# Moving a whole filter network, four d-tiles' transposes and two weight loads ahead of the first modulation

## The chip, the core and the metric

The kernel runs on one core of one Trainium2 chip. The metric is device microseconds of that core. PE is TensorE (PEld its weight loads), DVE is VectorE, ACT is ScalarE, POOL is GpSimd, SP is SyncE, which here only issues DMAs. All times below are in microseconds (us) unless ns is written.

## What is computed

Two layers over 512 latent tokens and 256 context tokens of width 1024. The first is a Hyena layer: a modulated norm, an input projection to four streams of 2048 channels, a short convolution, a long convolution by FFT with an implicit filter that a small network makes, a gate, and an output projection. The second is grouped-query attention. Cut to what this change touches:

```
sh, sc, gt = split(silu(c) @ ada_w[i] + ada_b[i], 3)
h_lat = rms_norm(x_lat, norm_g[i]) * (1 + sc) + sh          # the same for the context with c_ctx
proj  = h @ w_in                                            # (L, 1024) @ (1024, 8192)
h = sin(freq * (z @ w1 + b1)); h = sin(freq * (h @ w2 + b2)); h = sin(freq * (h @ w3 + b3))
k = (h @ w4) * decay                                        # 768 rows of z: the lags of both sequences
y = irfft(rfft(x1 * v) * rfft(k / sum|k|)); y = (y + u * d) * x0 * silu(z)
```

## The kernel before

Channels lie on partitions, tokens on the free axis: d-tile k holds 128 of the 1024 model channels for 512 + 256 tokens. Every product of two full-precision operands is split into a rounded high part and a remainder, and made of three matmuls (high by high, high by low, low by high). So `in_step` takes one d-tile of the projection with six matmuls: three of 512 latent columns (`pl`) and three of 256 context columns (`pc`).

The order of work is the order in which the code is written, sorted by a scheduler that gives each engine one fixed list; no engine passes an instruction that waits. `issue_after` (in `after`) only orders two instructions.

The start of the program does this. Small inputs come as rows (4 loads on SP, 15 on POOL's queue, `zt` among them) and are turned on PE (`ptr`). SP then loads two pieces of the modulation's weights, the 12 half tiles of x and ctx, and the other pieces. `load_x` also squares a half tile on ACT for the norm. `mlp_layer(li)` is one layer of the filter's network: a matmul, seven DVE operations over 768 columns of 64 partitions in two pieces (`ma`, `mn`), and a sine on ACT. Layer 0 runs at the start; layers 1 and 2 run inside `begin`. `ada0(dh, k)` are the matmuls of half dh of the modulation's columns (`prow`); `ada0_cols` copies them (`srow`), turns them (`padc`) and adds the bias (`ada`, `gsc`).

`begin` then writes the modulated d-tiles: for each k it turns x on PE (`xT`), applies scale and shift on ACT (`hf`), casts the latent high part on DVE and the context's on ACT, and subtracts for the low parts (`h_lo` on DVE, `hc_lo` on POOL). Two d-tiles behind, it runs `in_step` for two channel tiles, 16 (weights `whi`, `wlo`) and 32 (`fw`), with the second half of the modulation between. The low parts of weights are 1024 wide subtractions on POOL (`load_w`). The six `lags` of a group of 256 channels are the matmuls `pk` of the network's output by w4, multiplied by the decay on DVE into `kfl` and `kfc`.

After `begin`, eight groups g run: two `u_stage`, a `z_stage`, an `x0_stage` with the spectra's products (`ab..`, `Y..` on DVE, from PE's `pu`), a `z_stage`, and a last `x0_stage`, into whose eight steps the lags of group g + 1 are written:

```
x0_stage(g, 1, [none, fi[0], none, none, fi[1], fi[2], lambda: run(fi[3:5]), lambda: run(fi[5:7])])
```

`fi[1]` to `fi[6]` are the six lags. Tiles from `axt` (`xT`, `pk`, `pu`, `ks`, `pq`) share four PSUM banks in turn, so the fourth lag writes the bank of the last `pu`, which `ab..c` on DVE must have read. `ks` are the filter's DFTs (first `ks0m`); their operands F, Fh and Fl are made on POOL and ACT.

Of the kernel before, what the change touches and what calls it, by code (L numbers as in the profile page):

```python
# [19 lines left out]
P = 128  # L20
# [32 lines left out]
def hybrid_kernel(ctx: ExitStack, tc: tile.TileContext, x, c, ctxt, c_ctx, norm_g, ada_w, ada_b,  # L53
                  hy_w_in, hy_conv_w, hy_conv_b, fw1, fb1, fw2, fb2, fw3, fb3, fw4, freq, hy_d,
                  hy_w_out, at_w_in, at_q_g, at_k_g, at_w_out,
# [42 lines left out]
    lo_default, w_last = [G], [None]  # L98
# [8 lines left out]
    def load_w(src, shape, scale_row=None, lo_eng=None, st=None, more=None, behind=None):  # L107
# [14 lines left out]
        with after(behind) if behind else ExitStack():  # L122
            S.copy(hi, st)  # L123
# [6 lines left out]
    vb = gp.tile([P, NA + NB + NC_], F32, tag="vb", name="vb")  # L130
    conv_w_rows = hy_conv_w.rearrange("a k (t p) -> (a k t) p", p=P)
    conv_b_rows = hy_conv_b.rearrange("a (t p) -> (a t) p", p=P)
    d_rows = hy_d.rearrange("a (t p) -> (a t) p", p=P)
# [76 lines left out]
    hc_done = []  # L210

    def h_write(pt, s, k):

        hi, lo, w, en = (h_hi, h_lo, LL, V) if s == 0 else (hc_hi, hc_lo, LC, G)
        t = cvtile(f"hf_{s}_{k}")
        sa = S.activation(t[:, :w], pt[:, :w], AF.Identity, bias=col_sh(0, s, k), scale=col_gsc(0, s, k))
        if s:
            sa = S.copy(hi[:, k, :], t[:, :w])
        else:
            V.tensor_copy(hi[:, k, :], t[:, :w])  # L220
        r = en.tensor_tensor(lo[:, k, :], t[:, :w], f(hi[:, k, :]), ALU.subtract)
        if s:
            hc_done.append(r)
        return sa

# [15 lines left out]

    rows = hp.tile([P, T], F32, tag="y", name="rows")
    rowsA, rowsB, rowsC = rows[:, 0:P], rows[:, P:2 * P], rows[:, 2 * P:3 * P]
    nc.sync.dma_start(rowsA[16:24], c.rearrange("a (t p) -> (a t) p", p=P))
    nc.sync.dma_start(rowsA[24:32], c_ctx.rearrange("(t p) -> t p", p=P))
    nc.sync.dma_start(rowsA[0:16], norm_g.rearrange("l (t p) -> (l t) p", p=P))
    nc.sync.dma_start(rowsA[32:80], ada_b.rearrange("l (t p) -> (l t) p", p=P))
    zt = f(wp.tile([P, 1024], F32R, tag="wlo", name="zt", bufs=NWB))[0:33, 0:T]
    G.dma_start(zt, k_z)
    w1, w2, w3, bc = rows[0:33, 384:448], rows[0:64, 448:512], rows[0:64, 512:640], rows[:, 640:644]  # L250
    G.dma_start(w1, fw1[0])
    for i, b in ((0, fb1), (3, freq), (1, fb2), (2, fb3)):
# [12 lines left out]
    V.tensor_copy(vb[:, 0:NA], ptr[:, 0:NA])
# [17 lines left out]
    def mlp_layer(li, behind=None, pe_behind=None):  # L283

        w, cur, kdim, m = (w1, w2, w3)[li], feat[0], 64 if li else 33, P if li == 2 else 64
# [69 lines left out]
    def ada0(dh, k, behind=None):  # L355
# [3 lines left out]
        for x_, t in enumerate(ad_st.pop((dh, k))):  # L359
            q = (k % 2 * 2 + x_) * 32  # L360
            with after(behind) if behind else ExitStack():
                TE.matmul(prow[dh][q:q + 32, :], silp[:, 2 * k:2 * k + 32], t, start=k < 2, stop=k >= KD - 2)

    def ada0_cols(dh, behind=None):
        srow = cvtile(f"srow{dh}")
        sr = S.copy(srow[:, 0:512], prow[dh])
# [1047 lines left out]
```

## Time and profile before

| | |
|---|---|
| three timed runs | 1491.02 median, 1490.41 to 1492.36 |
| the profiled execution, timed | 1493.28 |
| its span in the profile | 1491.5 |
| PE busy | 1443.6 (97%) |
| DVE, ACT, POOL busy | 1086.2, 560.4, 500.1 |

The span is the time from the first to the last instruction of the profiled execution; its timed value has 1.8 around that. PE's busy time holds some waiting of pipelined matmuls. PEclk is the clock that TensorE was granted, as a share of its full speed. Rows below give the start, then the length, both in us, then engine, line, operation, what is written and what is read; in brackets stands the idle time of that engine just before, and what ended it.

### The profile page before, as it was taken

The numbers are of one execution on the slowest core, as the hardware profiler recorded it, in microseconds if no ns is written. First come the engines' busy times: TensorE is split into PE (matmuls) and PEld (weight loads), VectorE is DVE, ScalarE is ACT, GpSimd is POOL, SyncE is SP. The second block draws the span as 40 slices with busy tenths as digits, with TensorE's granted clock in tenths as the row PEclk, the third lists the DMA queues.
The fourth block names the chain that finished last, engine by engine and source line by source line (L and its number), as shares of the span: only waits on it lengthen the run. The fifth ranks groups of instructions, "written<-read, shape, count | busy, mean of one in ns | idle before, by whom it ended". The sixth has DMA issues, their size and how long they took to land.

```text
span 1491.5 us, 23805 instructions
## 1 busy us (share of the span) xinstructions
PE 1443.6 (97%) x9274; PEld 1260.5 (85%) x9274; DVE 1086.2 (73%) x1907; ACT 560.4 (38%) x1096; POOL 500.1 (34%) x452
## 2 busy tenths in 40 slices
PE   5799999999999999999999999999999999999998
PEld 2588888888888888888897878799998998998987
DVE  4668959678596785977858454656787878878886
ACT  5232332423323233232233343534445444445442
POOL 4363543635436255372554351211110000000005
PEclk9799999999999999999999999999999999999999
DMA  9511332323323233232222775255222312312111
GB/s 327 157 47 54 113 104 67 117 64 114 107 64 110 75 113 102 64 112 79 82 73 71 287 259 192 73 155 174 93 93 72 99 43 71 99 44 71 57 56 72
DMA packets 177601, 157.51 MB, mean 106 GB/s; under 512 B 7128, under 2 KB 155179, under 8 KB 176977
## 3 DMA queue, kind: packets, MB, share of 16 engines
q1 hardware_dynamic: 173136, 134.75, 29.4%
q0 software_dynamic: 4208, 20.72, 4.0%
q8 instruction: 73, 1.20, 0.3%
q10 hardware_dynamic: 144, 0.52, 0.1%
q14 instruction: 40, 0.32, 0.1%
HBM read 138.13 MB, written 17.84 MB: 105 GB/s over the span
## 4 chain that ended last, share of the span: by engine, by line
PE 72%; DVE 14%; DMA 2%; POOL 1%; issue 1%; ACT 1%; SPq 0%; ACTq 0%; POOLq 0%; DVEq 0%
PE po L71 3%; PE po L72 3%; PE po L70 3%; DVE Y L644 3%; PE et L1210 3%; PE pq L691 3%; PE plx L518 3%; PE plx L522 2%; PE plx L519 2%; PE px L70 2%; PE px L71 2%; PE px L72 2%; PE pq L70 2%; PE pq L72 2%; PE pq L71 2%; PE pz L71 2%
## 5 line engine op out<-in xcount | busy, mean ns | idle before, releaser
L124 POOL TENSOR_TENSOR wlo<-stg,whi 128x1024 fp32r<-128x1024 f32 x65 | 159.3, 2451 | 214.8 <-ACT whi L123 214.2
L123 ACT CAST whi<-stg 128x1024 fp32r<-128x1024 f32 x99 | 104.0, 1051 | 256.4 <-issue 180.5
L969 POOL TENSOR_TENSOR r2q<-s2q,mhalf 128x2 f32<-128x2 f32 x32 | 23.1, 722 | 343.8 <-DVE s2q L967 343.8
L1198 ACT ACTIVATE E<-sc,st 128x768 f32<-128x768 f32 x64 | 57.7, 902 | 127.0 <-DVE st L1196 126.9
L518 PE MATMUL plx<-h_hi,whi 128*128 128x512 f32 x248 | 101.2, 408 | 0.0
L522 PE MATMUL plx<-h_hi,wlo 128*128 128x512 f32 x248 | 98.3, 397 | 0.0
L519 PE MATMUL plx<-h_lo,whi 128*128 128x512 f32 x248 | 98.0, 395 | 0.0
L1195 DVE TENSOR_REDUCE st<-sc 128x1 f32<-128x768 f32 x64 | 61.0, 953 | 17.3 <-PE sc L72 17.0
L520 PE MATMUL pcx<-hc_hi,whi 128*128 128x256 f32 x248 | 69.8, 282 | 0.0
L521 PE MATMUL pcx<-hc_lo,whi 128*128 128x256 f32 x248 | 69.8, 281 | 0.0
L523 PE MATMUL pcx<-hc_hi,wlo 128*128 128x256 f32 x248 | 69.7, 281 | 0.0
L1215 DVE TENSOR_TENSOR ptl<-et,pth 128x768 fp32r<-128x768 f32 x64 | 61.0, 954 | 5.2 <-ACT pth L1214 3.2
L848 DVE TENSOR_TENSOR yl<-yf,yh 128x768 fp32r<-128x768 f32 x26 | 26.0, 1002 | 52.2 <-ACT yh L847 51.8
L1214 ACT CAST pth<-et 128x768 fp32r<-128x768 f32 x64 | 51.1, 799 | 31.1 <-PE et L1210 31.0
L520 PEld LDWEIGHTS pcx<-hc_hi,whi 128*128 128x128 f32 x248 | 46.8, 189 | 11.4
L521 PEld LDWEIGHTS pcx<-hc_lo,whi 128*128 128x128 f32 x248 | 46.8, 189 | 11.0
L72 PE MATMUL po<-pth,kvt 128*128 128x256 f32 x192 | 54.1, 282 | 0.0
L70 PE MATMUL po<-pth,kvt 128*128 128x256 f32 x192 | 54.1, 282 | 0.0
L71 PE MATMUL po<-ptl,kvt 128*128 128x256 f32 x192 | 53.9, 281 | 0.0
L518 PEld LDWEIGHTS plx<-h_hi,whi 128*128 128x128 f32 x248 | 46.9, 189 | 8.2 <-issue 0.2
L1210 PE MATMUL et<-ident,E 128*128 128x128 f32 x384 | 52.3, 272 | 0.0
L518 PE MATMUL plz<-h_hi,whi 128*128 128x512 f32 x128 | 52.0, 406 | 0.0
(917 smaller groups left out, 5124.1 us busy)
## 6 DMA issues: line engine op xcount, KB each, us to landing
stg<-in_hy_w_in_dram SPq DMA_DIRECT2D x64, 512.0 KB, 4.2
stg<-in_at_w_in_dram SPq DMA_DIRECT2D x40, 512.0 KB, 4.3
adw<-in_ada_w_dram SPq DMA_DIRECT2D x32, 512.0 KB, 3.9
yf<-y_scr POOLq DMA_DIRECT2D x32, 384.0 KB, 5.3
stg<-in_hy_w_out_dram SPq DMA_DIRECT2D x16, 512.0 KB, 6.7
stg<-in_at_w_out_dram SPq DMA_DIRECT2D x16, 512.0 KB, 3.5
dec<-in_k_dec_dram SPq DMA_DIRECT2D x48, 128.0 KB, 2.5
y_scr<-y SPq DMA_DIRECT2D x16, 384.0 KB, 3.2
```

What stands on the lines that cost most here:

```text
L70: TE.matmul(ps, lh, rh, start=first, stop=False)
L71: TE.matmul(ps, lh, rl, start=False, stop=False)
L72: TE.matmul(ps, ll, rh, start=False, stop=last)
L123: S.copy(hi, st)
L124: (lo_eng or lo_default[0]).tensor_tensor(lo, st, f(hi), ALU.subtract)
L518: TE.matmul(pl, hi[:, k, :], h_hi[:, k, :], start=fi, stop=False)
L519: TE.matmul(pl, hi[:, k, :], h_lo[:, k, :], start=False, stop=False)
L520: TE.matmul(pc[:, 0:LC], hi[:, k, :], hc_hi[:, k, :], start=fi, stop=False)
L521: TE.matmul(pc[:, 0:LC], hi[:, k, :], hc_lo[:, k, :], start=False, stop=False)
L522: TE.matmul(pl, lo[:, k, :], h_hi[:, k, :], start=False, stop=la)
L523: return TE.matmul(pc[:, 0:LC], lo[:, k, :], hc_hi[:, k, :], start=False, stop=la)
L1210: TE.transpose(tp_[:, b * P:(b + 1) * P], E[:, b * P:(b + 1) * P], ident)
```

## The change

- Small inputs: the host hands in `cols` (all vectors as columns, 128x292) and `fws` (the network's three weights), and with the positions `zt` three loads on SP take the place of the 19; the turning on PE goes.
- Loads on SP: all of x and ctx first, then the first half of the modulation's weights with the weights of channel tile 16 inside, then those of tile 32, w4 of group 0, and the second half.
- The network: layers 0 and 1 put their 768 columns as 384 columns on 128 partitions (two matmuls side by side on PE, one DVE operation where there were two). All three layers run before the modulation's columns are made.
- `keep_x` turns d-tiles 0 to 3 before the modulation is known and keeps them raw in SBUF; scale and shift are then applied in place. The first weights are cast to their high part before the columns, too.
- The context's high part is cast on DVE, not on ACT.
- `begin` runs the second tile one d-tile behind the first, with the rest of the modulation between.
- For group 0, the filter's DFTs and sums are ordered behind other work (by `after`).
- Of the six lags of each later group, the last two move into the next group's first stage (words 4 and 5 of `steps`), and the four others come one in each step.

```diff
-    hc_done = []
-    def h_write(pt, s, k):
-        hi, lo, w, en = (h_hi, h_lo, LL, V) if s == 0 else (hc_hi, hc_lo, LC, G)
-        t = cvtile(f"hf_{s}_{k}")
-        sa = S.activation(t[:, :w], pt[:, :w], AF.Identity, bias=col_sh(0, s, k), scale=col_gsc(0, s, k))
-        if s:
-            sa = S.copy(hi[:, k, :], t[:, :w])
-        else:
-            V.tensor_copy(hi[:, k, :], t[:, :w])
-        r = en.tensor_tensor(lo[:, k, :], t[:, :w], f(hi[:, k, :]), ALU.subtract)
-        if s:
-            hc_done.append(r)
+    hc_done, u_done = [], []
+    def h_write(k, src, behind=None):
+        t = raw.get(k)
+        if t is None:
+            t = cvtile(f"hf{k}")
+        for s, hi, lo, c_, en in ((0, h_hi, h_lo, slice(0, LL), V), (1, hc_hi, hc_lo, slice(LL, T), G)):
+            with after(behind) if behind else ExitStack():
+                sa = S.activation(t[:, c_], src(s), AF.Identity, bias=col_sh(0, s, k), scale=col_gsc(0, s, k))
+            V.tensor_copy(hi[:, k, :], t[:, c_])
+            r = en.tensor_tensor(lo[:, k, :], t[:, c_], f(hi[:, k, :]), ALU.subtract)
+        hc_done.append(r)
         return sa
+    raw = {}
...
-    nc.sync.dma_start(rowsA[16:24], c.rearrange("a (t p) -> (a t) p", p=P))
...
+    nc.sync.dma_start(vb, cols)
...
+    fw = hp.tile([P, T], F32, tag="y", name="fw")[:, 0:256]
+    nc.sync.dma_start(fw, fws)
+    nc.sync.dma_start(zt, k_z)
+    sil_done = S.activation(sil, vb[:, 16:32], AF.Silu)
...
-    def mlp_layer(li, behind=None, pe_behind=None):
...
+    def mlp_layer(li, behind=None, v_behind=None):
+        cur, m = feat[0], P if li == 2 else 64
...
-        for lo_, hi_ in ((0, 512), (512, 768)):
-            pp = axt(f"mlp{li}_{lo_}")
-            with after(pe_behind) if pe_behind else ExitStack():
-                mm = TE.matmul(pp[:m, 0:hi_ - lo_], w[:kdim, :m], cur[:kdim, lo_:hi_], start=True, stop=True)
-            aa, nn = a[:m, lo_:hi_], n[:m, lo_:hi_]
-            V.tensor_scalar(aa, pp[:m, 0:hi_ - lo_], bc[:m, li:li + 1], bc[:m, 3:4], ALU.add, ALU.mult)
+        for hh in range(2):
+            if li == 2 or not hh:
+                pp = axt(f"mlp{li}_{hh}")
+            r_ = slice(hh * 64, hh * 64 + 64)
+            lh, rh = ((fw[0:33, 0:64], cur[:, hh * 384:hh * 384 + 384]) if li == 0 else
+                      (fw[r_, 64 * li:64 * li + m], cur[r_, 0:384]))
+            mm = TE.matmul(pp[0:m, 0:384] if li == 2 else pp[r_, 0:384], lh, rh, start=True, stop=True)
+            if li < 2 and not hh:
+                continue
+            o_ = slice(hh * 384, hh * 384 + 384) if li == 2 else slice(0, 384)
+            aa, nn = a[:, o_], n[:, o_]
+            with after(v_behind) if v_behind else ExitStack():
+                V.tensor_scalar(aa, pp[:, 0:384], bc[:, li:li + 1], bc[:, 3:4], ALU.add, ALU.mult)
...
+    def turn_x(k):
+        pts = [axt(f"xT{k}_{s}") for s in range(2)]
+        for s, pt in enumerate(pts):
+            for t in range(4 if s == 0 else 2):
+                src = halves[(t + 4 * s) * 2 + k // 4][:, (k % 4) * P:(k % 4 + 1) * P]
+                TE.transpose(pt[:, t * P:(t + 1) * P], src, ident)
+        return pts
+    def keep_x(k):
+        t = raw[k] = cvtile(f"raw{k}")
+        pts = turn_x(k)
+        V.tensor_copy(t[:, LL:T], pts[1][:, 0:LC])
+        return S.copy(t[:, 0:LL], pts[0])
...
+    for i in range(12):
+        load_x(i)
+    for k in range(6):
         ada0_load(0, k)
-    sqs = [load_x(i, None if i else sil_done) for i in range(8)]
+    st16 = wp.tile([P, 1024], F32, tag="stg", name="stg16", bufs=NST)
+    nc.sync.dma_start(st16.rearrange("p (k e) -> p k e", k=KD), load_first(16))
+    for k in range(6, KD):
+        ada0_load(0, k)
+    st32 = wp.tile([P, 1024], F32, tag="stg", name="stg32", bufs=NST)
+    nc.sync.dma_start(st32.rearrange("p (k e) -> p k e", k=KD), load_first(32))
+    w4s0 = load_w4(0)
+    for k in range(KD):
+        ada0_load(1, k)
+    sqs = [square_x(i, None if i else sil_done) for i in range(6)]
     _, l0, s0 = mlp_layer(0, sqs[-1])
-    sqs += [load_x(i, None if i > 8 else s0) for i in range(8, 12)]
-    for k in range(2, KD):
-        ada0_load(0, k)
-    for k in range(2):
-        ada0(0, k)
+    sqs += [square_x(i, s0) for i in range(6, 10)]
+    m1, l1, s1 = mlp_layer(1, sqs[-1], l0)
+    sqs += [square_x(i, s1) for i in range(10, 12)]
     sv = ss.rearrange("p (t i) -> p t i", i=2)
-    with after(l0):
+    with after(l1):
         V.tensor_tensor(sv[:, :, 0], sv[:, :, 0], sv[:, :, 1], ALU.add)
     r0 = rms_rstd(sv[:, :, 0], 6, "r0", kg)
+    for k in range(2):
+        ada0(0, k, m1)
     for i in range(12):
         if i % 2:
             xs = S.activation(halves[i], halves[i], AF.Copy, scale=r0[:, i // 2:i // 2 + 1])
         else:
-            V.tensor_scalar(halves[i], halves[i], r0[:, i // 2:i // 2 + 1], None, ALU.mult)
+            xv = V.tensor_scalar(halves[i], halves[i], r0[:, i // 2:i // 2 + 1], None, ALU.mult)
+    m2, l2, s2 = mlp_layer(2)
     for k in range(2, KD):
+        if k < 6:
+            kx = keep_x(k - 2)
         ada0(0, k)
...
+    first_w = {16: load_w(None, (KD, P), st=st16, behind=kx)}
+    sr = ada0_cols(0, s2=s2)
...
-        AHEAD, sa, lags = 2, None, []
-        for k0_ in (0, 4):
-            for i in range(4 + AHEAD):
-                k = k0_ + i
-                if k == 1:
-                    ws.append(load_w(None, (KD, P), st=st32, behind=sa,
-                                     more=lambda i: [hp.tile([P, 1024], F32R, tag="AB", name=f"fw{x}", bufs=NAB)
-                                                     for x in range(2)]))
...
-                if i >= AHEAD:
-                    for e, w in zip(es, ws):
-                        last = in_step(w, *begun[e], k - AHEAD)
-                    if k0_ == 0:
-                        for k1 in (2 * (i - AHEAD), 2 * (i - AHEAD) + 1):
-                            ada0(1, k1, last)
-                if k0_ == 0 and i > 3:
-                    mlp_layer(i - 3, sa, last)
-                if k0_ and i:
-                    for _ in range(1 if i < 5 else 2):
-                        lags.pop(0)()
-            if k0_ == 0:
-                ada0_cols(1)
...
-                first_w[17] = load_w(hy_w[:, 17 * P:18 * P].rearrange("(k p) e -> p k e", p=P), (KD, P), behind=sa)
-                lags += kfilter(0, sa)
+        ws.append(load_w(None, (KD, P), st=st32, behind=sr,
+                         more=lambda i: [hp.tile([P, 1024], F32R, tag="AB", name=f"fw{x}", bufs=NAB) for x in range(2)]))
+        fw_cast, lags, pts = w_cast[0], [], {}
+        def write(k):
+            if k in raw:
+                return h_write(k, lambda s: raw[k][:, 0:LL] if s == 0 else raw[k][:, LL:T], None if k else fw_cast)
+            if k not in pts:
+                pts[k] = turn_x(k)
+            return h_write(k, lambda s: pts[k][s][:, 0:LL if s == 0 else LC])
+        for i in range(5):
+            if i < 4:
+                sa = write(i)
+            for e, w, k in zip(es, ws, (i, i - 1)):
+                if 0 <= k < 4:
+                    cur[0] = in_step(w, *begun[e], k, cur[0])
+            for k1 in ((0, 1), (2, 3), (4, 5), (6,), (7,))[i]:
+                cur[0] = ada0(1, k1, cur[0])
+            if i == 1:
+                lags += kfilter(0, sa, w4s0)
+        for _ in range(2):
+            lags.pop(0)(cur[0])
+        ada0_cols(1)
+        pts[4] = turn_x(4)
+        for i in range(6):
+            if i < 4:
+                sa = write(4 + i)
+            if i == 1:
+                first_w[17] = load_w(load_first(17), (KD, P), behind=sa)
+            for e, w, k in zip(es, ws, (i - 1, i - 2)):
+                if 0 <= k < 4:
+                    cur[0] = in_step(w, *begun[e], 4 + k)
+            if i and lags:
+                lags.pop(0)()
...
-    steps = (("m - y - - a - -", "- - Mp - Y - a -", "- - Po - - a - -", "- n Oc - N - a -", "- - C - a - - -"),
+    steps = (("m 4 y 5 - a - -", "- - Mp - Y - a -", "- - Po - - a - -", "- n Oc - N - a -", "- - C - a - - -"),
...
-        x0_stage(g, 1, [none, fi[0], none, none, fi[1], fi[2], lambda: run(fi[3:5]), lambda: run(fi[5:7])])
+        x0_stage(g, 1, [none, fi[0], none, none] + fi[1:5])
+        late += fi[5:]
```

On PE, this is before: layer 2 of the network (`mlp`) stands behind the second half of the modulation (`prow`), inside `begin`, and the columns (`padc`) behind it.

```order
L362 MATMUL prow_363<-ad_7_0_291,silp 32x512
L362 MATMUL prow_363<-ad_7_1_292,silp 32x512
L291 MATMUL mlp_0_456<-ma_416,rows 128x512
L291 MATMUL mlp_512_466<-ma_416,rows 128x256
L369 MATMUL padc_482<-sel_131,srow_480 128x4 x4
L565 MATMUL ptr_491<-ident,rows 128x128
```

And this is the start of PE's list now; `prow_239` is the first half of the modulation, `xT_0_283` the first kept d-tile.

```order
L275 MATMUL mlp_0_205<-zt,fw 64x384 x2
L275 MATMUL mlp_0_222<-ma_203,fw 64x384 x2
L352 MATMUL prow_239<-ad_0_139,silp 32x512 x2
L275 MATMUL mlp_0_258<-ma_220,fw 128x384
L275 MATMUL mlp_1_268<-ma_220,fw 128x384
L352 MATMUL prow_239<-ad_1_141,silp 32x512 x2
L352 MATMUL prow_239<-ad_2_0_143,silp 32x512
L352 MATMUL prow_239<-ad_2_1_144,silp 32x512
L378 MATMUL xT_0_283<-ident,x_117 128x128
```

All three layers have moved ahead of nearly the whole first half, and the transposes stand between its pieces.

On ACT, the rows around the first modulated d-tiles before (`srow_253` is the copy of the first half's columns):

```order
L366 COPY srow_253<-prow_220 128x512
L216 ACTIVATE hf_0_304<-xT_0_299,ada_83,gsc_85 128x512
L123 CAST whi_265<-stg_264 128x1024
L216 ACTIVATE hf_0_311<-xT_1_308,ada_83,gsc_85 128x256
L216 ACTIVATE hf_1_324<-xT_0_319,ada_83,gsc_85 128x512
```

and now (`ma_256` are the two sines of layer 2):

```order
L386 COPY raw_282<-xT_0_283 128x512
L288 ACTIVATE ma_256<-ma_256 128x384
L386 COPY raw_295<-xT_0_296 128x512
L386 COPY raw_308<-xT_0_309 128x512
L288 ACTIVATE ma_256<-ma_256 128x384
L386 COPY raw_321<-xT_0_322 128x512
L121 CAST whi_338<-stg_159 128x1024
L358 COPY srow_342<-prow_239 128x512
L217 ACTIVATE raw_295<-raw_295,ada_83,gsc_85 128x512
L121 CAST fw_357<-stg_169 128x1024
L217 ACTIVATE raw_282<-raw_282,ada_83,gsc_85 128x512
```

The copy of the columns now stands behind layer 2's sines, the four raw copies and the first weight cast; d-tile 0 (`raw_282`) is modulated behind the cast of the second weights.

At the end of a group, PE's list had the third and the fourth lag together ahead of the last d-tile of the projection:

```order
L432 MATMUL pk_2_1329<-w4h_1279,h_135 128x512
L433 MATMUL pk_2_1329<-w4l_1280,h_135 128x512
L432 MATMUL pk_3_1336<-w4h_1279,h_135 128x512
L433 MATMUL pk_3_1336<-w4l_1280,h_135 128x512
L518 MATMUL plx_1_1262<-h_hi,whi_1257 128x512
L519 MATMUL plx_1_1262<-h_lo,whi_1257 128x512
```

and has the fourth behind it now:

```order
L461 MATMUL pk_2_1288<-w4h_1238,h_116 128x512
L462 MATMUL pk_2_1288<-w4l_1239,h_116 128x512
L551 MATMUL plx_1_1221<-h_hi,whi_1216 128x512
L552 MATMUL plx_1_1221<-h_lo,whi_1216 128x512
L553 MATMUL pcx_1_1222<-hc_hi,whi_1216 128x256
L554 MATMUL pcx_1_1222<-hc_lo,whi_1216 128x256
L555 MATMUL plx_1_1221<-h_hi,wlo_1217 128x512
L556 MATMUL pcx_1_1222<-hc_hi,wlo_1217 128x256
L461 MATMUL pk_3_1301<-w4h_1238,h_116 128x512
```

So six matmuls of the projection now lie between the two lags.

## Rows read from the trace of the kernel before

**Rows 1.** The page: busy us of each engine, share of the span, instructions.

```profile
PE 1443.6 (97%) x9274; PEld 1260.5 (85%) x9274; DVE 1086.2 (73%) x1907; ACT 560.4 (38%) x1096; POOL 500.1 (34%) x452
```

**Rows 2.** Busy us by stretch: PE, PEld, DVE, ACT, POOL; granted clock, DMA, GB/s.

```profile
50.70:53.70 3.00, 0.05 (x5) 0.01 (x1) 2.47 (x7) 1.80 (x4) 1.58 (x1) 1.00 0.28 75
53.70:74.10 20.40, 15.46 (x49) 11.44 (x50) 15.23 (x29) 6.71 (x13) 6.03 (x5) 0.50 0.20 59
74.10:82.90 8.80, 8.80 (x51) 7.68 (x51) 5.62 (x7) 4.45 (x8) 4.28 (x6) 0.99 0.16 46
82.90:122.10 39.20, 35.29 (x213) 31.24 (x212) 26.57 (x42) 14.06 (x23) 27.88 (x25) 0.96 0.19 55
153.30:1491.50 1338.20, 1321.02 (x8631) 1168.69 (x8631) 986.08 (x1747) 504.26 (x991) 431.23 (x380) 1.00 0.33 101
```

**Rows 3.** PE's waits over the span: us in total, times, longest.

```profile
PE ptr L263 <- DMA rows<-in_ada_b_dram: 4.5, 1, 4.5
PE mlp L291 <- ACT ma L300: 3.0, 1, 3.0
PE pk L432 <- DVE ab21c L635: 1.1, 1, 1.1
```

**Rows 4.** Timeline, the start of the program.

```profile
7.40 2.79 PE L291 MATMUL mlp<-zt,rows 33*64 33x512 f32 x4 [2.55 <-DMA rows<-in_hy_fw_dram]
10.03 1.25 DVE L293 TENSOR_SCALAR ma<-mlp,rows 64x512 f32<-64x512 f32 x2 [4.69 <-DMA rows<-in_hy_freq_dram]
...
15.61 0.61 DVE L298 TENSOR_SCALAR ma<-ma 64x512 f32<-64x512 f32 x2
...
16.95 0.92 ACT L300 ACTIVATE ma<-ma 64x512 f32<-64x512 f32 x2
...
19.26 0.63 ACT L322 ACTIVATE sq<-xutl 128x512 f32<-128x512 f32 x1
...
20.77 0.17 DVE L392 TENSOR_TENSOR ss<-ss 128x6 f32<-128x6 f32 x1 [4.54 <-ACT sq L322]
...
22.71 1.28 DVE L398 TENSOR_SCALAR x<-x,r 128x512 f32<-128x512 f32 x3 [1.57 <-POOL r L207]
...
25.18 1.32 ACT L396 ACTIVATE xutl<-xutl,r 128x512 f32<-128x512 f32 x2
...
27.79 0.58 ACT L366 COPY srow<-prow 128x512 f32<-128x512 f32 x1 [1.29 <-PE prow L362]
...
30.01 0.78 ACT L216 ACTIVATE hf<-xT,ada,gsc 128x512 f32<-128x512 f32 x1 [1.64 <-PE xT L548]
...
30.69 1.04 ACT L123 CAST whi<-stg 128x1024 fp32r<-128x1024 f32 x1
...
31.29 0.69 DVE L221 TENSOR_TENSOR h_lo<-hf,h_hi 128x512 fp32r<-128x512 f32 x1
...
31.78 0.50 PE L518 MATMUL pl<-h_hi,whi 128*128 128x512 f32 x1 [0.28 <-ACT whi L123]
```

**Rows 5.** Timeline, POOL and DVE at the split of the second weights.

```profile
34.17 0.93 POOL L221 TENSOR_TENSOR hc_lo<-hf,hc_hi 128x256 fp32r<-128x256 f32 x1
...
35.05 2.82 POOL L124 TENSOR_TENSOR fw<-stg,fw 128x1024 fp32r<-128x1024 f32 x1
...
35.56 2.59 DVE L220 CAST h_hi<-hf 128x512 fp32r<-128x512 f32 x1
```

**Rows 6.** Timeline of PE in begin.

```profile
47.38 0.50 PE L518 MATMUL pl<-h_hi,whi 128*128 128x512 f32 x1
...
49.67 1.07 PE L362 MATMUL prow<-ad,silp 128*32 128x512 f32 x8
...
69.47 0.79 PE L519 MATMUL pl<-h_lo,whi 128*128 128x512 f32 x1 [1.13 <-DVE h_lo L221]
```

**Rows 7.** Timeline at the end of group 0: PE, then DVE.

```profile
153.26 0.50 PE L432 MATMUL pk<-w4h,h 128*128 128x512 f32 x1 [1.04 <-DVE ab01c L635]
...
151.99 1.22 DVE L635 TENSOR_TENSOR ab01c<-pu,kt0c 128x1024 f32<-128x1024 f32 x1
```

More of the change, by code (lines that the diff above doesn't have):

```diff
@@ L361, in ada0, with ada0_cols @@
             with after(behind) if behind else ExitStack():
-                TE.matmul(prow[dh][q:q + 32, :], silp[:, 2 * k:2 * k + 32], t, start=k < 2, stop=k >= KD - 2)
-    def ada0_cols(dh, behind=None):
+                mm = TE.matmul(prow[dh][q:q + 32, :], silp[:, 2 * k:2 * k + 32], t, start=k < 2, stop=k >= KD - 2)
+        return mm
+    def ada0_cols(dh, behind=None, s2=None):
         srow = cvtile(f"srow{dh}")
-        sr = S.copy(srow[:, 0:512], prow[dh])
+        with after(s2) if s2 else ExitStack():
+            sr = S.copy(srow[:, 0:512], prow[dh])
         padc = axt(f"padc{dh}")
@@ L425, in kfilter, with lags @@
         kfs[g] = (kl, kc)
-        def lags(tl):
+        def lags(tl, behind=None):
             dc = k0.tile([P, 256], F32, tag="dec", name=f"dec{g}_{tl}", bufs=2)
@@ L431, in lags @@
             hs = h3[:, tl * P:(tl + 1) * P]
-            TE.matmul(pk, hs, wh, start=True, stop=False)
+            with after(behind) if behind else ExitStack():
+                TE.matmul(pk, hs, wh, start=True, stop=False)
             TE.matmul(pk, hs, wl, start=False, stop=True)
@@ L439, in lags @@
                 V.memset(dst[0:1, 256:512], 0.0)
-        return [lambda tl=tl: lags(tl) for tl in range(6)]
+        return [lambda behind=None, tl=tl: lags(tl, behind) for tl in range(6)]
     def knorm(g):
@@ L447, in knorm @@
             mx = kg.tile([P, 256], F32, tag="mx", name=f"mx{g}_{si}", bufs=2)
-            V.tensor_reduce(mx, src.rearrange("p a (s c) -> p c (a s)", s=2), AX.X, ALU.add,
-                            apply_absolute_value=True)
+            with after(u_done[0]) if not g else ExitStack():
+                V.tensor_reduce(mx, src.rearrange("p a (s c) -> p c (a s)", s=2), AX.X, ALU.add,
+                                apply_absolute_value=True)
             mxs.append(mx)
@@ L480, in kdft @@
                 c0, c1, d0, d1 = src[:, hf], src[:, hb], src[:, hf], src[:, hb]
-            G.tensor_tensor(F[:, 0:256], c0, c1, ALU.add)
-            G.tensor_tensor(F[:, 256:512], d0, d1, ALU.subtract)
+            with after(hc_done[-1]) if not g else ExitStack():
+                G.tensor_tensor(F[:, 0:256], c0, c1, ALU.add)
+                G.tensor_tensor(F[:, 256:512], d0, d1, ALU.subtract)
             if nm == "p" and par == 0:
@@ L497, in finish @@
                     Fh, Fl = banks[par]
-                    mm3(pt[:, r_], kmat[0][:, mset, par, cs, :], kmat[1][:, mset, par, cs, :],
-                        Fh[:, r_], Fl[:, r_], True, True)
+                    with after(cur[0]) if not g else ExitStack():
+                        mm3(pt[:, r_], kmat[0][:, mset, par, cs, :], kmat[1][:, mset, par, cs, :],
+                            Fh[:, r_], Fl[:, r_], True, True)
                 pts.append(pt)
@@ L514, in hybrid_kernel, with in_step @@
     hy_w = hy_w_in[0]
-    def in_step(w, pl, pc, k):
+    def in_step(w, pl, pc, k, behind=None):
         (hi, lo), fi, la = w, k == 0, k == KD - 1
-        TE.matmul(pl, hi[:, k, :], h_hi[:, k, :], start=fi, stop=False)
+        with after(behind) if behind else ExitStack():
+            TE.matmul(pl, hi[:, k, :], h_hi[:, k, :], start=fi, stop=False)
         TE.matmul(pl, hi[:, k, :], h_lo[:, k, :], start=False, stop=False)
@@ L527, in spread @@
             it()
-    begun = {}
+    begun, cur = {}, [None]
     def begin(es):
@@ L577, in in_proj @@
         for k in range(KD):
[L578 removed]
+            cur[0] = in_step(w, pl, pc, k)
             spread(items, k)
@@ L776, in slots @@
             table = {"n": kn[0], "N": kn[1], "a": ada_next, "-": none, "y": lambda: [y() for y in ya],
-                     "Y": lambda: [y() for y in yb]}
+                     "Y": lambda: [y() for y in yb], "4": lambda: late.pop(0)(), "5": lambda: late.pop(0)()}
             for i in range(4):
```

95 lines of the change are left out of this document (34 added, 61 removed).

## Prediction

> **What bounds the kernel now.** Read the page first: PE is busy 1443.6 of 1491.5 us [rows 1], so it bounds the kernel, and only its 47.9 idle and its time at a low clock can be won; no edit here takes much work from it. Then the table of stretches [rows 2]: behind 153.3 PE idles 17.2 of 1338.2 us, so the rest, about 30.7, lies in the start. There the reader sees three holes. PE stands still from 50.7 to 53.7, its clock falls to 0.50 and stays there to 74.1, and inside that it idles another 4.9; from 82.9 to 122.1 it idles 3.9. Then the waits [rows 3]: the hole at 50.7 is layer 2 of the network, waiting for layer 1's sine, and behind the start the one wait that repeats is that of the fourth lag for `ab..c`, about 1.1 us, one for each of the seven groups that prepare a next one. So two questions decide: when does PE reach a common point (I take the first matmul of group 0's x0 stage, where the stretch of [rows 2] ends at 122.1; behind it both kernels have the same work), and what becomes of the seven waits.
>
> **1. Layers 0 and 1.** The network can start when the third load on SP has landed. Before, PE's first wait ended at 4.5 with the fourth small load on that queue [rows 3]; I take 4.5. A layer's matmuls took 2.8 for 768 columns [rows 4]. Now two pieces of 384 columns write different halves of PSUM's partitions. If they run together, they take 1.4, if in turn 2.8. The nearest row is the modulation's, where four full-precision matmuls (two records each) of 512 columns that write four strips take 1.07 together [rows 6], so I take 1.4. DVE's seven steps over 768 columns ran from 10.0 to 16.2 [rows 4], half as many columns 3.1; a sine takes 0.46, hand-overs 0.3. Layer 0 ends at 4.5 + 5.3 = 9.8, layer 1 at 15.0 or so.
> The Trainium skill (TensorEngine Tiling (Array Packing), Key Properties) says that different tiles of the array execute in parallel, but also that changing the tiling mode drains the engine. With the first alone the layers take 1.4 each, in turn 2.8 each and the sum below would be 2.8 worse; no row of before shows two half arrays.
>
> **2. The norm.** The last two squares now wait for layer 1's sine on ACT. Two took 1.5 (19.26 to 20.77 [rows 4]): 16.5. But DVE's list has both first steps of layer 2 (0.63 each) around the sum of squares, and the second needs the second matmul, at 15.0 + 2.8 = 17.8. So the norm's factor starts at 18.5, and from the sum to the first scaling were 1.94 (20.77 to 22.71), so 1.75 more: scaling starts at 20.2, against 22.71. DVE scales six half tiles at 0.43, to 22.8; ACT six, which took 3.8 (22.71 to 26.50), to 24.0.
>
> **3. ACT becomes the path.** Layer 2's first sine waits for 3.5 of DVE work behind the scalings: 26.3. Behind it in ACT's list stand another sine, three raw copies (0.58, as `srow`), and the first weight cast (1.04): the columns' copy starts at 30.0, not at 27.79. The modulation's matmuls, which the loads held up before, are done by then. From that copy to the first modulated tile took 2.2 (27.79 to 30.01), so 32.2.
>
> **4. The first matmul.** ACT now modulates d-tile 1 (0.78), casts the second weights (1.04), then modulates d-tile 0 (0.78): 34.8. DVE's cast of it then meets POOL's split of those weights, begun at 34.1. In the row of before such a cast took 2.59 and ended with POOL's 2.82 [rows 5]; a pass of that width not held takes 0.43 (the scalings [rows 4]). I take the held one: `in_step` starts at 36.9 (35.2 if not held), 5.1 later than before (31.78).
> The Trainium skill (SBUF — State Buffer, on the shared port pair) says the pair is an exclusive lock for a whole instruction. It speaks against the change, which also gives DVE the context's casts; by it the eight new casts may each wait for a POOL split, which my sum takes once, and once in step 6.
>
> **5. First half of begin.** d-tile 0 also needs DVE's subtraction (0.69 [rows 4]), the context's cast (0.3, an estimate from 0.43 for twice its columns) and POOL's subtraction (0.93 [rows 5]): its six matmuls end at 39.1. Then seven `in_step` at 1.15 (two between 47.38 and 49.67 [rows 6]) and four groups of `prow` at 1.0: 51.1. PE has idled from about 31 to 36.9, and before, 3.0 of idling were followed by the clock of 0.50, which came back at 74.1, after 4.6 us of dense work from 69.47 [rows 2, 6]. So 4.6 us at half rate cost 2.3: 53.4. Before, this point was 50.7; the change is 2.7 behind here.
>
> **6. Second half of begin.** From 50.7 to 82.9 PE did 0.05 + 15.46 / 2 + 8.80 = 16.6 us of work at full clock [rows 2], of which 1.4 was layer 2 (half of layer 0's 2.8, an estimate), now done. 15.2 remain, and 1.5 for POOL's split of tile 17's weights, which stands ahead of d-tile 5's `hc_lo` in POOL's list: 70.1, against 82.9. Between the halves the columns' copy, `padc`, a modulated tile and its cast follow on each other, 2.2 + 0.78 + 0.43 = 3.4; PE has two lags, `padc` and two d-tiles' transposes meanwhile, so I count no hole; without that cover it is 3.4.
>
> **7. To the x0 stage.** From 82.9 to 122.1 PE was busy 35.3; the DFTs now come seven d-tiles later, which gives POOL and ACT the time to make their operands. I leave 0.8 for one wait of the old kind: 106.2 against 122.1. The start gives **15.9**.
>
> **8. The lags.** PE was free at 152.2, `ab01c` ended at 153.2, and the fourth lag began at 153.26 [rows 7]. With one `in_step` (1.05 to 1.15) ahead of it the wait is 0.1 at most. The last two lags come among the next stage's matmuls, in banks that DVE left long before; each of the six later groups gains alike: **7.0**. The loads of decay for them are issued when DVE leaves their buffers, as before.
>
> The sum is 22.9 from the profiled execution's 1493.3, which gives 1470.4. The median lies 2.3 below that execution, so I predict **1468**. The other edits cost or give nothing that I can see: 16 loads fewer, since SP's stream of large loads ends ahead of steps 3 to 5; w4's earlier load; the order among group 0's DFTs, for which PE has work of the projection.
>
> **Bounds.** Up: no fall of the clock 2.3, no held cast 1.8, no wait at tile 17 1.5 and none in step 7 0.8, the lags whole 0.6, so 7.0 better: 1461. Down: the layers' matmuls in turn 2.8, two more casts held 4.8, half of the lags' gain lost 3.5, so 11.1 worse: 1479.
>
> **Rivals.**
> - *DVE and POOL bind begin.* POOL's splits and `w4l` stand among the `hc_lo`, and DVE has more casts. For it: 4.9 idle in the old second half, waiting for such tiles. Against it: DVE needs 0.43 + 0.69 + 0.3 for a d-tile, PE 2.3. One more hold of 2.4 for each of three splits gives 1475, with the other low bounds up to 1480.
> - *The lags only move their wait.* DVE's products end just when the wait ends [rows 7], so they are as late for whatever needs them next. Then only the start is won: 1475. Against it: the banks behind the fourth lag's go to `pq` and the moved lags, the first of them two `in_step` later.
> - *The start is better still,* if neither clock nor cast holds it: 1461 by the bounds, and down to 1455 where begin packs closer than its old rows.
> - *Slower: the clock stays low.* From 36.9 to 70.1 PE has 27 us of work at full rate, with small pieces between. At half rate through all of it the start costs 25 more than I count, which cancels the gain; beyond that point, into the 35 us of step 7, the kernel is slower, 1503 if ten more go so. For it: the row of 53.7 to 74.1, where 15.46 of 20.4 were busy and the clock stayed down. Against it: what ran there was little but layer 2, columns, transposes and waits, and 4.6 us of `in_step` brought it back. The Trainium skill (TensorE: Matmul & The Clock Gate, Part 1) says the same of idling and of sustained work.
>
> **How the numbers follow.** My forecast, 1463 to 1474, has 0.55. Bound begin or a moved wait (1474 to 1482) has 0.27, the better start 0.13, a low clock through begin and on 0.03, no effect 0.02. From 1460 to 1480 leaves out some 0.06 below and 0.09 above. A measurement of this kernel tells 0.2%, 3 us, from no change: faster 0.95, same 0.02, slower 0.03.
>
> **What would show it.** In the new profile: layer 1's sine ends near 15; scaling starts near 20; the first `in_step` near 37, behind a DVE cast that ends with POOL's split; clock 0.50 from the thirties to the early forties; the first DFT `ks0m` near 78 without a long wait; the x0 stage's first matmul near 106; no wait of `pk` for `ab..c` over 0.2. I am wrong if PE waits for `hc_lo` or `h_lo` through begin, if the clock stays down beyond 45, or if another wait of about 1 us stands once in each group.

## The result: 13.6 us slower

The changed kernel took 1504.31 us (median of four runs, 1502.51 to 1507.34) against 1490.72 before: ratio 1.0092, with a 95% interval of 1.0072 to 1.0113. The forecast was 1468, faster. The profiled execution took 1507.34, with a span of 1505.6 us.

The page of the changed kernel, the line that answers to [rows 1]:

```profile
PE 1447.3 (96%) x9271; PEld 1261.5 (84%) x9271; DVE 1083.9 (72%) x1903; ACT 560.5 (37%) x1090; POOL 489.1 (32%) x437
```

PE now idles 58.3 us, not 47.9, and is busy 3.7 longer with three records fewer; the stretches at the lower clock, shown below, account for that. Its waits show where it idles (us in total, times, longest):

```profile
PE adap L187 <- DVE y L736: 18.0, 6, 3.7
PE pl L551 <- DVE h_hi L218: 6.7, 1, 6.7
PE mlp L275 <- ACT ma L288: 5.3, 1, 5.3
...
PE plx L551 <- DVE cvx L625: 2.5, 1, 2.5
```

The seven waits of `pk` for `ab..c` [rows 3] are gone, as forecast. In their place stands the first row: `adap`, a product of two columns for the second layer's modulation, waits for DVE's reading of the inverse transform, 3 us on average in six groups. Where the loss grows can be read from one filter DFT of each group, the last of group 0 and the first of the others (first PE start in the views of the tiles `ks0c`, `ks1m`, `ks4m`, `ks7m`; the last two columns are the kernel of the third experiment):

| | before | changed | difference | lags ahead of y | difference |
|---|---|---|---|---|---|
| group 0, `ks0c` | 118.0 | 112.4 | -5.6 | 112.6 | -5.4 |
| group 1 | 170.8 | 164.2 | -6.6 | 164.3 | -6.5 |
| group 4 | 452.4 | 453.2 | +0.8 | 442.7 | -9.7 |
| group 7 | 733.9 | 749.5 | +15.6 | 721.1 | -12.8 |

So the start gains 5.6 where 15.9 were forecast (the x0 stage's first matmul begins at 116.54, not at 106.2), and from the mark of group 1 to that of group 7 the kernel loses 22.2 where 6 were to be won.

The wait, in the timeline of the changed kernel around one of these places (PE, then DVE, then ACT):

```profile
244.49 2.84 PE L726 MATMUL pq<-kinv,Y 128*128 128x128 f32 x24
...
250.89 0.64 PE L179 MATMUL adar<-adw,silp 128*32 128x128 f32 x16
253.97 0.35 PE L187 MATMUL adap<-sel,adr 128*128 128x2 f32 x2 [2.44 <-DVE y L736]
...
249.41 3.64 DVE L478 TENSOR_REDUCE mx<-kfl 128x256 f32<-128x2048 f32 x1
252.98 0.45 DVE L735 SCALAR_TENSOR_TENSOR y<-pq,rn,qs 128x256 f32<-128x256 f32 x1
253.37 0.46 DVE L736 SCALAR_TENSOR_TENSOR y<-pq,rn,qs 128x256 f32<-128x256 f32 x1
253.76 0.67 DVE L464 TENSOR_TENSOR kfc<-pk,dec 128x512 f32<-128x512 f32 x1
...
252.43 0.47 ACT L734 ACTIVATE qs<-pq,rn 128x256 f32<-128x256 f32 x1
```

`pq` is done by 247, but DVE reads it only from 253, behind a 3.6 us reduction and ACT's `qs`. In itself that costs nothing: `y` is needed much later. But `axt` has four banks in turn, and the first stage now takes lag 5 (bank A), `pq` (B, C), lag 6 (D), `adar` (A), `adap` (B). So `adap` gets `pq`'s first bank. Before, without the two lags ahead of and behind `pq`, it got the bank of the sixth lag.

And most of the waits have a second price (windows of the changed kernel: us, PE busy, PEld, DVE, ACT, POOL, then the granted clock, DMA share and GB/s):

```profile
37.10:41.40 4.30, 0.03 (x1) 0.03 (x1) 3.16 (x4) 4.30 (x7) 2.38 (x1) 0.50 1.06 367
41.40:47.30 5.90, 5.90 (x19) 3.21 (x20) 5.83 (x9) 1.79 (x4) 4.74 (x5) 0.50 0.24 61
77.40:80.00 2.60, 0.17 (x2) 0.00 (x0) 2.10 (x4) 1.78 (x4) 2.52 (x4) 1.00 0.00 0
81.50:84.90 3.40, 3.40 (x14) 3.08 (x13) 3.30 (x6) 0.00 (x0) 3.32 (x4) 0.50 0.59 159
...
251.50:254.00 2.50, 0.06 (x5) 0.06 (x1) 2.50 (x4) 1.05 (x3) 1.69 (x3) 1.00 0.23 71
255.60:259.00 3.40, 3.40 (x13) 2.92 (x12) 3.40 (x4) 2.18 (x3) 1.37 (x2) 0.50 0.66 189
...
447.00:450.00 3.00, 2.39 (x14) 2.15 (x15) 3.00 (x6) 0.78 (x3) 2.29 (x4) 1.00 0.16 48
...
641.30:648.10 6.80, 6.16 (x20) 5.32 (x21) 5.84 (x10) 2.79 (x5) 2.12 (x4) 0.50 0.42 127
```

The wait of the last row but one ended at 447.61 and had lasted 2.47. That of the last row ended here:

```profile
641.94 0.56 PE L187 MATMUL adap<-sel,adr 128*128 128x2 f32 x2 [3.51 <-DVE y L736]
```

The clock falls to 0.50 at five of the six waits (that of 447.61 is the exception). At three it falls behind the wait, 0.1 to 1.7 us after its end, so that it is low while PE works without a break, and it stays low for 3.4 us. At the last two it falls while PE still waits, 0.7 and 1.0 us ahead of the end, and stays low for 6.8. The five stretches (one of each kind shown) hold 22.2 us of busy PE, so up to 11.1 are lost, beside the 18.0 of waiting. The third experiment's kernel bears this out: with the same 9271 records, its PE is busy 1435.6, which is 11.7 less.

### The profile page after: what moved, and what is told of

Read it like the earlier page. It is cut to its first block, busy times and chain, and to the rows that moved or that the text cites. A ratio compares the mean times of both kernels' runs of the same rounds, so it can differ in the third digit from the quotient of the medians.

```text
span 1505.6 us, 23751 instructions
## 1 busy us (share of the span) xinstructions
PE 1447.3 (96%) x9271; PEld 1261.5 (84%) x9271; DVE 1083.9 (72%) x1903; ACT 560.5 (37%) x1090; POOL 489.1 (32%) x437
## 5 line engine op out<-in xcount | busy, mean ns | idle before, releaser
L1233 DVE TENSOR_REDUCE st<-sc 128x1 f32<-128x768 f32 x64 | 61.0, 953 | 16.7 <-PE sc L70 16.3
```

## The experiments

**The groups.** Theory A: the late lags shift the rotation, and `adap` waits for the bank of `y`. Theory B: the start's other order does it. Theory A': DVE is late for any bank. The first four ran on one chip, beside the kernel before at 1491.24.

*Lags back in the changed kernel.*

```diff
-    steps = (("m 4 y 5 - a - -", ...
+    steps = (("m - y - - a - -", ...
-        x0_stage(g, 1, [none, fi[0], none, none] + fi[1:5])
-        late += fi[5:]
+        x0_stage(g, 1, [none, fi[0], none, none, fi[1], fi[2], lambda: run(fi[3:5]), lambda: run(fi[5:7])])
```

> The changed kernel with the lags placed as before: none in the next group's first stage, the third and fourth and the fifth and sixth in pairs in the last two steps. Theory A (the late lags shift which PSUM bank the modulation's product adap gets, so PE waits 3.0 us for y in six groups, and its clock falls behind each wait): adap's waits (18.0 us in six) are gone, the clock is at its high level behind group 0's start, the old wait for ab..c (1.1 us, seven times) is back, and the time is that of the start alone, 5.6 us under before: 1485. Theory B (the loss behind group 1 comes from the changed start, by the order of loads or of products on DVE): adap's waits stay, 1500 or more.

Measured: 1485.88, ratio 0.9965 (0.9951 to 0.9978), as theory A said. The clock is high from 48.5 to 801. No `adap` stands among the waits, and the old wait is back, as in this row (there are seven like it):

```profile
PE pk L461 <- DVE ab51c L670: 1.1, 1, 1.1
```

*Late lags alone, in the kernel before* (the same edit the other way round).

> The kernel before with one part of the change: the last two lags of each later group in the next group's first stage, the others one in each step. Theory A: the waits for ab..c go (1.0 us in seven places), adap waits about 3 us for y in six groups with a lower clock behind it, so 28 us are lost and 7 won: about 1512. Theory B: no such wait, 1484.

Measured: 1508.40, ratio 1.0118 (1.0098 to 1.0138). Its waits:

```profile
PE adap L189 <- DVE y L701: 16.7, 6, 3.5
```

The clock falls at five of the six here too. So the loss needs nothing of the new start: B is out.

*Both lags ahead of y.*

```diff
-    steps = (("m 4 y 5 - a - -", ...
+    steps = (("m 4 5 y - a - -", ...
```

> The changed kernel with the two late lags one behind the other ahead of the inverse transform (steps 1 and 2, the transform in step 3, adap as before in step 5). adap then writes the bank of the sixth lag, whose product now stands ahead of the long reduction in DVE's list. Theory A (bank): no wait of adap over 0.3 us, no fall of the clock behind group 1, both gains are kept: 1490.7 - 5.6 - 7 = 1478. Theory A' (DVE is as late for any bank, because two products and a reduction now stand ahead of y): adap waits 2 us or more again, 1498 or more.

Measured: 1477.76, ratio 0.9907 (0.9894 to 0.9921). The same place in its timeline (PE, then DVE):

```profile
246.12 2.84 PE L726 MATMUL pq<-kinv,Y 128*128 128x128 f32 x24
250.98 0.65 PE L179 MATMUL adar<-adw,silp 128*32 128x128 f32 x16
251.55 0.38 PE L187 MATMUL adap<-sel,adr 128*128 128x2 f32 x2
...
249.52 0.61 DVE L464 TENSOR_TENSOR kfc<-pk,dec 128x512 f32<-128x512 f32 x1
250.07 3.85 DVE L478 TENSOR_REDUCE mx<-kfl 128x256 f32<-128x2048 f32 x1
253.85 0.46 DVE L735 SCALAR_TENSOR_TENSOR y<-pq,rn,qs 128x256 f32<-128x256 f32 x1
254.24 0.46 DVE L736 SCALAR_TENSOR_TENSOR y<-pq,rn,qs 128x256 f32<-128x256 f32 x1
```

DVE reads `pq` as late as before, 2.3 us behind `adap`'s start, and PE does not wait: `adap` now has the bank of the sixth lag, which DVE read at 249.5. The same holds in the five groups behind this one (`y` begins 2.2 to 3.6 us behind `adap`), and no wait of `adap` stands in the run's list. That decides between A and A'. Both gains of the change are then kept: 1.0 for each group, and the start.

*No bank of its own for adap.* It writes two free columns of the bank that `adar` gets.

```diff
-    def ada_rows(t, nm):
+    def ada_rows(t, nm, end):
         pt = axt(f"adar{nm}")
+        end(pt)
...
-        pt, c_ = axt(f"adap{nm}"), o0 // P
-        TE.matmul(pt[:, 0:2], r, sel, start=True, stop=True)
+        pt, c_ = (axt(f"adap{nm}") if pt is None else pt)[:, P:P + 2], o0 // P
+        TE.matmul(pt, r, sel, start=True, stop=True)
...
-                r = ada_rows(adw.pop(0), f"_{l}_{o0}")
+                r = ada_rows(adw.pop(0), f"_{l}_{o0}", lambda pt: n and ada_end(*pieces[n - 1], box.pop(), "", pt))
...
```

> The changed kernel, lags and transform in the same steps, but adap takes no bank of its own: it writes two free columns of the bank that the next piece's adar gets in the same step, which is the fifth lag's. Only the bank differs from the changed kernel. Theory A (bank): no wait of PE for y's reading of pq in any group, clock high behind group 1, 1478. Theory A' (DVE's or ACT's lateness itself, whatever the bank): a wait of 2 us or more stays at this place, for kfc or adr, 1495 or more.

Measured: 1530.33, ratio 1.0262 (1.0248 to 1.0276). The time lies where A' put it (1495 or more), but the wait is one that neither theory named:

```profile
PE adar L180 <- DVE ada L189: 38.7, 13, 5.6
```

The wait for `y` is gone, but the edit put a new one there: `adar` shares its tile with `adap` now, so it waits until DVE has read those two columns, and that reading stands in the same late list. As a test of the bank it is inconclusive.

*The piece of the modulation two steps later*, `adap` still in `pq`'s bank, on another chip (before: 1490.56).

```diff
-    steps = (("m 4 y 5 - a - -", ...
+    steps = (("m 4 y 5 - - - a", ...
```

> The changed kernel with the modulation's piece (adar, adap) two steps later in the group's first stage, at step 7, and nothing else moved: adap still gets the bank that y reads. Theory A (PE waits for that bank and for nothing else): PE comes 2.1 us later to the same event, so the wait of 3.0 shrinks to 0.9 or less in six groups and the falls of the clock behind it go: 1490.7 - 5.6 - 7 + 5 = about 1483 or a little less. Rival (the reader slides along with PE, since DVE's own list is what is late): waits of 2.5 us or more stay, 1500.

Measured: 1485.15, ratio 0.9962 (0.9950 to 0.9975). Its waits:

```profile
PE adap L187 <- DVE y L736: 4.9, 6, 1.7
```

The waits shrink to 0.8 on average, and the clock stays high from 84.3 to 800 us. That is theory A's account and not the rival's (2.5 or more), but not all of it: four waits are 0.3 to 0.6, the last two 1.60 and 1.69 where at most 0.9 was expected, and the time is 2 longer than A's 1483.

**The start.** Four edits, each alone on top of the kernel with both lags ahead of `y` (its x0 products begin at 119.8, `ab000a` on DVE, and this is the point compared), on one chip with before at 1491.67.

*The network's casts behind the d-tiles.*

```diff
-            V.tensor_copy(h3t, a)
-            V.tensor_copy(h3[0:64], f(h3t[0:64]))
-            ve = V.tensor_tensor(h3[64:128], a[64:128], f(h3t[64:128]), ALU.subtract)
...
+            feat.append(h3_write)
...
```

`h3_write` holds the same three and is called behind d-tile 3's casts.

> The kernel with both lags ahead of y, and with the three DVE casts of the network's output put behind the first four d-tiles' casts instead of ahead of the columns' sums. Theory H (these casts, 4.2 us of DVE of which the forecast counted nothing, held the columns back): padc ends at 34.7 as before, the columns' sums follow at once instead of at 36.4, and the first in_step begins 1.6 us earlier than 41.4; the x0 stage of group 0 begins 1.6 us earlier. Rival (POOL's splits are what holds, and the casts only fill a gap): the first in_step stays within 0.5 of 41.4.

Measured: 1476.47, ratio 0.9900 (0.9887 to 0.9912); x0 products at 118.2, 1.6 earlier. In its timeline DVE takes the columns when `padc` ends; the split still holds the cast of d-tile 0:

```profile
35.18 0.24 DVE L373 TENSOR_TENSOR ada<-padc,vb 128x8 f32<-128x8 f32 x2 [2.52 <-PE padc L366]
...
38.58 2.00 DVE L218 CAST h_hi<-raw 128x512 fp32r<-128x512 f32 x1 [0.50 <-ACT raw L217]
```

The first `in_step` came at 40.63, 0.9 earlier than the base's 41.51 and not 1.6, since this run's `padc` was 0.3 later and the columns' last sum took longer. H holds, with 0.9 from the casts. The other 0.7 goes with the clock: its low stretch behind the idling held 4.4 us of busy PE and not 5.7, and half of that difference is 0.7.

*Whole pairs in the modulation's second half.*

```diff
-            for k1 in ((0, 1), (2, 3), (4, 5), (6,), (7,))[i]:
+            for k1 in ((0, 1), (2, 3), (4, 5), (6, 7), ())[i]:
...
-        TE.matmul(pc[:, 0:LC], hi[:, k, :], hc_hi[:, k, :], start=fi, stop=False)
+        with after(behind) if behind else ExitStack():
+            TE.matmul(pc[:, 0:LC], hi[:, k, :], hc_hi[:, k, :], start=fi, stop=False)
```

> The same base, with the last two pieces of the modulation's second half together in one step (four strips at a time) and no matmul of the projection allowed between the four of a pair. Theory P (two strips alone take as long as four): begin's first half ends 2.0 us earlier, since two lone pieces at 1.05 and one broken pair at 2.1 become two whole pairs at 1.07. Rival (strips add up, as matmuls in turn would): no change there.

Measured: 1475.54, ratio 0.9891 (0.9878 to 0.9904); x0 products at 117.5, 2.3 earlier. The rows of `prow` in the changed kernel's timeline (two records are one matmul; four matmuls fill the four strips)

```profile
48.78 1.07 PE L352 MATMUL prow<-ad,silp 128*32 128x512 f32 x8
52.08 1.06 PE L352 MATMUL prow<-ad,silp 128*32 128x512 f32 x6
53.07 0.38 PE L553 MATMUL pc<-hc_hi,whi 128*128 128x256 f32 x1
53.39 1.04 PE L352 MATMUL prow<-ad,silp 128*32 128x512 f32 x2
56.55 1.05 PE L352 MATMUL prow<-ad,silp 128*32 128x512 f32 x4
58.78 1.05 PE L352 MATMUL prow<-ad,silp 128*32 128x512 f32 x4
```

show that one, two, three or four matmuls take the same 1.05 us, if nothing stands between them. Here the matmul `pc` cut a pair in two. With whole pairs the five rows of `prow` become three.

*Group 0's last two lags behind begin.*

```diff
-            if i and lags:
+            if i and (i > 4 or len(lags) > 2):
                 lags.pop(0)()
+                if i > 4:
+                    lags.pop(0)()
```

> The same base, with group 0's last two lags behind the last in_step of begin rather than between the d-tiles. Theory C (PE waits 2.5 us there for the first tile's bank, which ACT and DVE have yet to read; anything put there is free): 0.95 of the wait is covered, and the fall of the clock behind it, 3.4 us at half rate, may go: 1 to 2.7 us earlier at the x0 stage. Rival (the lags' products on DVE, which then come later, push the bank's readers or the filter's DFTs back by as much): no gain, the wait of 2.5 stays or moves to ks0m.

Measured: 1474.21, ratio 0.9885 (0.9872 to 0.9898); x0 products at 116.7, 3.1 earlier, more than expected. A wait and a window of it:

```profile
PE plx L551 <- DVE cvx L627: 0.8, 1, 0.8
```

```profile
80.00:83.40 3.40, 3.40 (x23) 3.00 (x22) 3.33 (x7) 0.00 (x0) 3.32 (x3) 1.00 0.19 52
```

The wait at the end of `begin` is 0.8 and not 2.5, and the clock does not fall behind it (compare 81.50 to 84.90 above). C holds for the wait. The part that the fall has in the 3.1 is less sure: in the kernel with the lags back, whose start is the same as the base's, a wait of 2.5 at this place was followed by no fall, and its x0 products began at 118.8, 1.0 ahead of the base.

*D-tile 0 ahead of the second weights' cast.*

```diff
-                return h_write(k, ..., None if k else fw_cast)
+                return h_write(k, ..., None)
```

> The same base, with d-tile 0 modulated ahead of the cast of the second weights instead of behind it. Theory F (d-tile 0's cast is held by POOL's split of those weights because it comes after their cast): its cast takes 0.45 and not 2.0, ends at 38.2 instead of 41.4, and the first in_step begins at 38.3. PE then reaches the second tile's first in_step about 3 us earlier and waits there for fw's split: 0 to 3 us earlier at the x0 stage. Rival (the held cast only changes places: another cast waits for the split instead, and PE waits for that): no gain.

Measured: 1482.03 (1476.43 to 1482.88), ratio 0.9928 (0.9915 to 0.9940); in the profiled execution, which took 1482.21, x0 products at 123.2, 3.4 later. Neither expectation had a loss. The first `in_step` began at 39.59, 1.9 earlier. But its timeline (DVE, then PE) has

```profile
40.55 2.10 DVE L218 CAST hc_hi<-raw 128x256 fp32r<-128x256 f32 x1 [0.29 <-ACT raw L217]
...
44.35 1.92 PE L352 MATMUL prow<-ad,silp 128*32 128x512 f32 x4
47.57 1.92 PE L352 MATMUL prow<-ad,silp 128*32 128x512 f32 x4
51.16 1.05 PE L352 MATMUL prow<-ad,silp 128*32 128x512 f32 x4
```

the split holding the context's cast instead, and the modulation in eight pieces, the first two at half clock; `padc` was 1.3 later too, in this run. The next two kernels go after the pieces.

*The first three together* (before: 1490.56).

> Both lags ahead of y, the network's casts behind the first d-tiles, whole pairs in the modulation, and group 0's last two lags behind begin, together. Each alone began the x0 stage of group 0 1.6, 2.3 and 3.1 us earlier than the base. If they are independent: 7.0 earlier than the base's 119.8 to 112.8, and 1477.8 - 7.0 = 1471. If the last (the cover of one wait) is worth its 3.1 only once and the others shift what it covers: 4 to 5, 1473.

Measured: **1469.72**, ratio 0.9858 (0.9845 to 0.9872); x0 products at 113.0, 6.8 earlier than the base, where 7.0 were expected. The three add up.

> The same four together with d-tile 0 ahead of the cast of the second weights, which alone was 3.4 us slower. Theory Q (it was slower because the earlier start broke the modulation's second half into eight lone pieces of 1.05 us, two of them at half clock; with whole pairs held together that can't come back): 0 to 2 us faster than without it, 1469 to 1471. Rival (it was slower because POOL's split then holds the context's cast, 2.1 us for 0.3): 1 to 3 us slower than without it.

Measured: 1470.45, ratio 0.9869 (0.9854 to 0.9884); x0 products at 112.4. Its first `in_step` came at 37.11, 3.5 earlier than without the fourth edit; 0.6 is left at the x0 stage. In its timeline the held cast is still there:

```profile
38.06 2.09 DVE L218 CAST hc_hi<-raw 128x256 fp32r<-128x256 f32 x1 [0.28 <-ACT raw L217]
```

In time the two kernels can't be told apart. Behind the first `in_step` this one loses 2.9 (3.5 less 0.6), where the edit alone lost 5.3 (1.9 and 3.4). By this estimate the broken pairs made nearly half of the loss; the held cast stands in what is left, but no run takes it away, so its share is not shown.

## Why the prediction was wrong, step by step

**Step 8 failed, and with it the sign.** The waits for `ab..c` went as forecast and 1.0 a group was won (the table's last column: 7.4 over seven). What failed is "the last two lags come among the next stage's matmuls, in banks that DVE left long before". That holds for the lags' own banks. It was not asked which tiles get the banks behind them. The rival "the lags only move their wait" named the mechanism, but looked only at "the banks behind the fourth lag's", stopped at `pq` and found no late reader; `adap`, four allocations behind, was not followed, and DVE's order there (`mx` ahead of `y`) was not read. Its price of 1475 counted a wait of the old size. The new one is 2.3 to 3.7 us long, and the clock falls at most of them, which the old 1.1 us never caused. Undone (1485.88), made alone (1508.40) and given another bank (1477.76), it is shown. Yet without it the forecast would have been missed too: 1477.76 lies above 1463 to 1474, because the start gave 5.6 and not 15.9. That shortfall is the failure of steps 1 to 7 below. Two of the prediction's own signs of being wrong came: the clock was low beyond 45, and a new wait stood in six groups.

**Steps 1 and 2: right in kind, 2.0 too early** (the scalings began at 22.20, not at 20.2). The two half arrays run together (a layer's four records took 1.54; 1.4 forecast, 2.8 in turn). The layers ended later, at 11.65 and 17.48 instead of 9.8 and 15.0:

```profile
11.14 0.51 ACT L288 ACTIVATE ma<-ma 128x384 f32<-128x384 f32 x1
...
16.96 0.52 ACT L288 ACTIVATE ma<-ma 128x384 f32<-128x384 f32 x1 [2.45 <-DVE ma L286]
...
33.00 0.59 ACT L358 COPY srow<-prow 128x512 f32<-128x512 f32 x1
33.18 2.34 POOL L122 TENSOR_TENSOR wlo<-stg,whi 128x1024 fp32r<-128x1024 f32 x1 [11.02 <-DMA ad<-in_ada_w_dram]
33.28 3.06 DVE L296 TENSOR_TENSOR h<-ma,h3t 64x768 fp32r<-64x768 f32 x1
36.37 0.24 DVE L368 TENSOR_TENSOR ada<-padc,vb 128x8 f32<-128x8 f32 x2
36.83 0.81 ACT L217 ACTIVATE raw<-raw,ada,gsc 128x512 f32<-128x512 f32 x1 [3.24 <-DVE gsc L369]
...
38.66 2.38 POOL L122 TENSOR_TENSOR fw<-stg,fw 128x1024 fp32r<-128x1024 f32 x1 [3.13 <-ACT fw L121]
39.33 1.99 DVE L218 CAST h_hi<-raw 128x512 fp32r<-128x512 f32 x1 [0.50 <-ACT raw L217]
41.37 0.80 PE L551 MATMUL pl<-h_hi,whi 128*128 128x512 f32 x1 [6.68 <-DVE h_hi L218]
```

(the changed kernel's start). Layer 0's sine stood behind a square on ACT, and DVE's seven steps took 3.6, not 3.1. **Step 3** was 4.6 late at the first modulated tile: the copy came at 33.0, not 30.0, and then DVE had the three casts of the network's output ahead of the columns, the third held for 3.06 by POOL's first split. They were not in the sum at all. **Step 4** had the held cast right (1.99; 2.59 taken), and so the first `in_step` is late by what steps 1 to 3 were: 4.5. The Trainium skill (SBUF — State Buffer, on the shared port pair) has the lock between DVE and GpSimd; the trace agrees, with casts of 0.43 (latent) and 0.3 (context) that took 1.99 to 2.10 where they began under a split of 2.4, in this kernel and in those above.

**Step 5** mis-sized the modulation: four groups of `prow` at 1.0 became six of 1.04 to 1.94 with the first at half clock. **Step 6** was nearly right: 17.6 from 59.8 to 77.4, where 16.7 were forecast. **Step 7** counted one wait of 0.8 and got 2.5 for `cvx`, the fall of the clock behind it, and 1.3 in two waits for `Fl0`. Of the 10.3 that the start lacks, 4.5 lie ahead of the first `in_step`, 1.9 in step 5, 0.9 in step 6 and 3.0 in step 7. The runs put sizes on three causes, 6.8 together, though the clock falling or not can move this point by itself (1.0 between two runs with the same start); the late layers and the copies, the rest, were only read from the trace and not tried.

**The rivals.** "The clock stays low" ended on the right side but for another reason, so that its 1503 is near the measured time by luck: the clock was back at 47.3, and what cost was the later waits and its fall at most of them.

## What to carry to other kernels

When an allocation moves into or out of a stage, write down the ring of buffers for the whole stage, with the last reader of each and its place in that reader's list; the wait appears at whoever comes one turn later, be it the least product of the kernel. And price a wait like these in a dense stretch at more than its length: here 3.0 of waiting cost 4.7 of time (the table's two differences are 28.4 apart at group 7, over six waits). A late reader that delays nobody (`y`) is a trap laid for the next change.

## What the hardware showed that was not expected

- Five of six waits of 2.33 to 3.71 us in a stretch where PE was otherwise busy went with 3.4 to 6.8 us at the 1.2 GHz level, which began between 1.0 us ahead of the wait's end and 1.7 us behind it. The wait of 2.47 did not, nor did waits of 1.1 us, or those of 0.8 on average (longest 1.7). The Trainium skill (TensorE: Matmul & The Clock Gate, Part 1) has idling and the lower level together; that a pause of 2.33 us can bring it, and one of 2.47 need not, is what these rows add.
- Matmuls of 512 columns into 32-column strips cost the same 1.05 us alone as four together, and a single other matmul between them ends the sharing (a group of four cut in two took 1.06 and 1.04).
